# First block's mixer: half of the convolution moved from VectorE to ScalarE and Pool, rotary embedding from Pool to VectorE, and another order of the projections

## The chip, the core and the metric

The kernel runs on one core of a Trainium2 chip. The metric is the device time of one execution in microseconds; the number shown for a version is the median of its runs. The core has five instruction queues that run in parallel and meet at semaphores: TensorE (PE, with its weight loads as PEld), VectorE (DVE), ScalarE (ACT), GpSimd (POOL, "Pool" in the text) and SyncE (SP), which issues the transfers.

## What is computed

Two transformer blocks, each of two layers, on 256 tokens of 1024 features, in float32. The change lies in the mixer of the first block, which every one of its two layers runs between two feed-forward networks (FFN):

```python
def first_block(x, ...):
    for l in range(DEPTH):                                   # DEPTH = 2
        x = x + 0.5 * swiglu(rms_norm(x, ffn1_norm[l]), ...)
        h = rms_norm(x, mix_norm[l]) @ w_in[l]
        u_pool = h[..., OFF_POOL:OFF_MOBA]                   # 256 columns
        qm, km, vm = jnp.split(h[..., OFF_MOBA:OFF_DIL], 3, axis=-1)
        qd, kd, vd = jnp.split(h[..., OFF_DIL:OFF_CONV], 3, axis=-1)
        u_conv = h[..., OFF_CONV:]                           # 512 columns: a, g
        y_pool = pool_mixer(u_pool, pool_w[l], pool_scale[l])
        qm = apply_rope(to_heads(qm, MOBA_HEADS), cos, sin)  # and km, qd, kd
        y_moba = moba_attention(qm, km, vm)
        y_dil = dilated_attention(qd, kd, vd)
        y_conv = conv_module(u_conv, conv_w[l], conv_b[l], conv_ln_g[l], conv_ln_b[l])
        mix = jnp.concatenate([y_pool, y_moba, y_dil, y_conv], axis=-1)
        x = x + mix @ w_out[l]
        x = x + 0.5 * swiglu(rms_norm(x, ffn2_norm[l]), ...)
```

`conv_module` gates 256 channels, `a * sigmoid(g)`, convolves each over the tokens with 31 taps of its own, and ends with a layer norm and a SiLU. `apply_rope` turns 16 of the 64 features of each head of q and k. `pool_mixer` takes running means over 2, 4, 8 and 16 tokens.

## The kernel before

Weights come in transfers of 1 MB into one of three buffers `raw`, issued by SP in the order of the program. Each is split into two exact parts for TensorE: ACT copies `hi` (L210), DVE subtracts to get `lo` (L211), two pieces of 128x1024 for each transfer. A product of two split operands is three matmuls (`mm3`, L221 to L223). In almost all of the program TensorE runs these back to back, and the two splits run one or two transfers ahead of it.

`mixer1` (one call for each layer) projects the normed tokens. The outputs a and g of the convolution (`pa`, `pgc`) and the pool columns (`pp`) come feature-major, 128 features by 256 tokens, in `fm_pair`: 48 matmuls of 256 columns each. q and k of the one attention, q and k of the other and the v of both come token-major in three calls of `qkv_part(0)`, `(1)`, `(2)`: 48 matmuls of 512 columns each into two banks `pq`, which ACT evicts into `qkv` (L440). All of them take one of four banks of the pool `mmm`.

`scores` does one attention: rotary embedding in place on `qkv` in six Pool operations (L449 to L454), transposes of q and k (`pqk`, L459) evicted by ACT into `qkT` (L460), score products `ps` (L471) for the first and then the second 128 queries, and the softmax: DVE adds the mask into `e` (L478) and takes the maximum (L479), ACT takes the exponential (L481), DVE divides (L483, L484), TensorE transposes the weights (`ppt`, L490) and ACT evicts them (L491). There are two pieces of `ps` in the bank pool `mta`, so the second group of score products waits until DVE has read the first.

`conv_module` works on `hc`, two halves j of 128 channels with 256 tokens and 30 zeros ahead. A tap is one DVE operation `yc = hc * w + yc` on 128x256 (L553 the first, L555 the others). Of the second half's 31 taps the first eight are taken off DVE: ACT makes the product `pr` (L544, the first one straight into `yp`) and Pool adds it into `yp` (L547), with three buffers for `pr`; DVE adds `yp` in the end (L556).

`pool_mix` scales `pp` into `up` on DVE (L508), builds the window sums by doubling on Pool (L510, L512, L514, L516; tiles `s2`, `s4`, `s8`, `s16`, all named `s` in the rows), makes the means `pl` on Pool and DVE (L525 to L527), and TensorE multiplies each group with its matrix (`pps`, L533).

After the three projections the output projection `po` runs over the mixed columns `mixT`, whose last two column tiles come from the convolution. `block1` calls FFN, mixer, FFN for each layer.

Calls stand in the order of the code, but the order of instructions on each engine is set by a scheduler when the program is built: it moves independent work of several calls together, and then each engine runs its own list in order. An engine whose next instruction waits does nothing else.

Of the kernel before, what the change touches and what calls it, by code (L numbers as in the profile page):

```python
# [21 lines left out]
NPOOL, PRB = 8, 3  # L22
# [58 lines left out]
def _fm(w, n0, n1):  # L81
    """chunks of 256 columns: [chunk, 128, K / 128, 256]"""
    w = np.asarray(w)[:, n0:n1]
    return w.reshape(-1, 128, (n1 - n0) // 256, 256).transpose(2, 1, 0, 3)


def _tm(w, n0, n1, width=512):
    """column blocks, each with all its contraction tiles: [block, 128, K / 128, width]"""
    w = np.asarray(w)[:, n0:n1]
    return w.reshape(-1, 128, (n1 - n0) // width, width).transpose(2, 1, 0, 3)  # L90


# columns of w_in: q and k of both attentions of the first block, then their v
# [3 lines left out]
def _layout(inputs):  # L97
    """Arrays as the launch takes them: weights in the blocks that one transfer loads,
    small vectors as columns, the others as they come."""
# [50 lines left out]
def _build(ctx, tc, nc, V, A, P, T, a, out, col, ccol, stop):  # L150
# [29 lines left out]
    def C(name):  # L180
        lo, hi = ccol[name]
        return cst[:, lo:hi]
# [12 lines left out]
    def load_w(src, split=2):  # L195
        """src: DRAM view [128, a, b]; returns its exact parts hi + lo, both fp32r."""
# [20 lines left out]
    def mm3(ps, l, r, li, ri, start, stop):  # L217
        """ps += l^T r with the three leading partial products of the split operands."""
# [14 lines left out]
    def rsqrt(v, n, root=1.0):  # L233
        """root / sqrt(v) for n columns: seed y from the exponent, times two quadratics in t = v y^2
        whose product follows t^-1/2 to 3e-8 over the range of the seed."""
# [14 lines left out]
    def rstd(ssum, n, count, eps):  # L250
        """1 / sqrt(ssum / count + eps)"""
# [19 lines left out]
    # ================= block 1 =================  # L271
    class Norm1:
        """xT <- (x * g)^T split, one half of the columns after the other"""
# [25 lines left out]
        def finish(self):  # L299
            """the halves still to do; returns r columns and r along the free axis on all partitions"""  # L300
# [11 lines left out]
    def fm_pair(mm, w, mcols, n, name):  # L312
        """two feature-major output tiles of n tokens in one bank; w: chunk [128, 8, 256]."""
# [11 lines left out]
    def ffn1(norm, nxt, wg, wu, wd, l, after_mixer, nside=0, early=None, between=None):  # L325
        with ExitStack() as st:
            work = pool("fwork", 2, stack=st, side="right")
            hp = pool("fh", 1, stack=st, side="right")
            # banks 0 and 1, 2 to 5: what comes next begins in banks that are free by then
# [42 lines left out]
    # rope tables of block 1, token-major [128, 2, 8]  # L372
# [31 lines left out]
    def mixer1(norm, nxt, l):  # L404
        w_fm, w_tm, w_out = a["w_in_fm"][l], a["w_in_tm"][l], a["w_out"][l]
        with ExitStack() as st:
# [8 lines left out]
            # projections that stay feature-major: conv (a, g), pool  # L415
# [13 lines left out]
            # token-major projections: q and k of each attention, then v of both  # L429
# [13 lines left out]
            def scores(qo, mask, name):  # L443
                """transposed softmax weights: queries 128: see keys 0:128 and 128:256, queries 0:128 only the first"""
# [4 lines left out]
                P.tensor_tensor(rt[0], t1, cb, op=ALU.mult)  # L449
                P.tensor_tensor(rt[1], t2, sb, op=ALU.mult)  # L450
                P.tensor_tensor(rt[2], t2, cb, op=ALU.mult)
                P.tensor_tensor(rt[3], t1, sb, op=ALU.mult)
                P.tensor_tensor(t1, rt[0], rt[1], op=ALU.subtract)
                P.tensor_tensor(t2, rt[2], rt[3], op=ALU.add)  # L454
# [84 lines left out]
            def conv_module():  # L539
                yc = keep.tile([128, 2, 256], F32, name="yc")  # L540
                yp = keep.tile([128, 256], F32, name="yp")
                for t in range(NPOOL):
                    pr = work.tile([128, 256], F32, name="pr", bufs=PRB)
                    A.activation(pr if t else yp, hc[:, 1, t:t + 256], AF.Copy,  # L544
                                 scale=pcol("conv_w", (l * 31 + t) * 2 + 1))
                    if t:
                        P.tensor_tensor(yp, yp, pr, op=ALU.add)  # L547
                for j, t0 in ((0, 0), (1, NPOOL)):
                    for t in range(t0, 31):
                        w = pcol("conv_w", (l * 31 + t) * 2 + j)  # L550
                        src = hc[:, j, t:t + 256]
                        if t == t0:
                            V.tensor_scalar(yc[:, j], src, w, None, op0=ALU.mult)  # L553
                        else:
                            V.scalar_tensor_tensor(yc[:, j], src, w, yc[:, j], op0=ALU.mult, op1=ALU.add)  # L555
                V.tensor_tensor(yc[:, 1], yc[:, 1], yp, op=ALU.add)  # L556
# [30 lines left out]
            qkv_part(0)  # L587
            pp = fm_pair(mm, load_w(w_fm[2]), 0, 256, "pp")
            pt_moba = scores(0, C("causal"), "m")
            qkv_part(1)  # L590
# [7 lines left out]
            # output projection  # L598
# [34 lines left out]
    def setup():  # L633
        """what the first products do not need, in two steps"""
# [16 lines left out]
    def ada(l, v):  # L651
        """vector v of layer l, step by step: columns [128, k, stream], or gate * g rows in DRAM."""
# [17 lines left out]
        # row 32 (ns j + s): half j of stream s  # L670
# [40 lines left out]
    def tick(n, l=0):  # L711
        """n steps of the modulation of layer l, in the shade of the products."""
# [26 lines left out]
    # ================= block 2 =================  # L739
# [649 lines left out]
```

## Time and profile before

| | before |
| --- | --- |
| runs, us | 1941.36, 1938.75, 1937.58 |
| median, us | 1938.75 |
| the profiled execution: span from its first to its last instruction, us | 1936.9 |
| TensorE busy | 1897.2 us, 98% of the span |
| DVE busy | 1365.2 us, 70% |
| ACT busy | 952.5 us, 49% |
| Pool busy | 52.5 us, 3% |
| mean granted TensorE clock | 0.992 of full speed |

The page of the profiled execution gives only its span as its own time; it stands 1.85 us under the median of the runs. Busy shares are means over stages with different limits; the pages' slices show the clock of TensorE below full speed in one slice only, so what happens in a mixer of about 102 us is to be read from the timelines and waits of that stretch.

### The profile page before, as it was taken

To read this page: it belongs to the slowest core of one execution; us is meant where nothing else is said; L and a number is where in the kernel's file an instruction comes from. 1 tells how busy PE (TensorE), PEld (TensorE's weight loads), DVE (VectorE), ACT (ScalarE), POOL (GpSimd) and SP (SyncE) were. 2 spreads that over 40 slices of the span, in tenths; PEclk is the share of its full clock that TensorE was granted. 3 is DMA by queue.
4 is the path that set the end of the run, shared out by engine and by line. 5 is a ranking of instruction groups with operands and counts; after the bars stand their busy time and mean duration, and the time that the engine had idled before them with its cause. 6 is when DMAs were issued, how large, how long until landed. Compare 5 with 4: busy or idle time off the path is not lost.

```text
span 1936.9 us, 28694 instructions
## 1 busy us (share of the span) xinstructions
PE 1897.2 (98%) x11658; PEld 1638.5 (85%) x11658; DVE 1365.2 (70%) x2169; ACT 952.5 (49%) x1518; POOL 52.5 (3%) x96
## 2 busy tenths in 40 slices
PE   8999999999999998999999999999999999989998
PEld 8997879997999786899888767888878777669997
DVE  7777797777677769765544475795785787757774
ACT  5443555443444355644543475642432466766652
POOL 0000210000000012000000000000000001000000
PEclk9999999999999999999999999999999999989999
DMA  8667525667566752555533221355564532115552
GB/s 313 241 215 241 182 96 194 227 224 265 192 225 214 261 174 87 189 181 178 181 136 131 88 71 66 104 177 192 187 210 146 188 114 92 45 55 196 183 180 95
DMA packets 57419, 326.20 MB, mean 168 GB/s; under 512 B 6460, under 2 KB 6716, under 8 KB 26568
## 3 DMA queue, kind: packets, MB, share of 16 engines
q1 hardware_dynamic: 57288, 324.38, 49.0%
q8 instruction: 91, 1.49, 0.3%
q14 instruction: 40, 0.33, 0.1%
HBM read 323.29 MB, written 1.07 MB: 167 GB/s over the span
## 4 chain that ended last, share of the span: by engine, by line
PE 90%; DVE 5%; ACT 3%; issue 1%; POOL 0%; DMA 0%; SPq 0%; DVEq 0%; ACTq 0%
PE pg L221 8%; PE pg L223 7%; PE pg L222 7%; PE py L221 4%; PE py L223 4%; PE py L222 4%; PE pu L223 4%; PE pu L221 4%; PE pu L222 4%; PE pa L221 3%; PE pa L222 3%; PE pa L223 3%; PE pyd L221 3%; PE pyd L223 3%; PE pyd L222 3%; DVE yc L555 2%
## 5 line engine op out<-in xcount | busy, mean ns | idle before, releaser
L210 ACT ACTIVATE hi<-raw 128x1024 fp32r<-128x1024 f32 (+1 forms) x506 | 511.2, 1036 | 599.7 <-issue 143.7
L211 DVE TENSOR_TENSOR lo<-raw,hi 128x1024 fp32r<-128x1024 f32 (+1 forms) x506 | 600.5, 1204 | 243.8 <-ACT hi L210 243.8
L223 PE MATMUL pg<-xTh,lo 128*128 128x256 f32 (+1 forms) x1072 | 321.6, 300 | 0.4 <-DVE lo L211 0.4
L221 PE MATMUL pg<-xTh,hi 128*128 128x256 f32 (+1 forms) x1072 | 321.7, 300 | 0.2
L222 PE MATMUL pg<-xTl,hi 128*128 128x256 f32 (+1 forms) x1072 | 321.0, 300 | 0.0
L221 PEld LDWEIGHTS pg<-xTh,hi 128*128 128x128 f32 x1072 | 205.8, 192 | 9.7 <-issue 2.5
L223 PEld LDWEIGHTS pg<-xTh,lo 128*128 128x128 f32 x1072 | 205.5, 192 | 7.0 <-DVE lo L211 0.7
L222 PEld LDWEIGHTS pg<-xTl,hi 128*128 128x128 f32 x1072 | 205.6, 192 | 6.3
L222 PE MATMUL pu<-xTl,hi 128*128 128x256 f32 x704 | 199.4, 283 | 0.0
L221 PE MATMUL pu<-xTh,hi 128*128 128x256 f32 x704 | 199.3, 283 | 0.0
L223 PE MATMUL pu<-xTh,lo 128*128 128x256 f32 x704 | 199.2, 283 | 0.0
L664 DVE SCALAR_TENSOR_TENSOR aacc<-raw,sc_c,aacc 128x1024 f32<-128x1024 f32 x140 | 174.1, 1278 | 0.2
L221 PE MATMUL py<-hi,hTh 128*128 128x512 f32 x352 | 140.2, 398 | 0.0
L222 PE MATMUL py<-lo,hTh 128*128 128x512 f32 x352 | 139.7, 397 | 0.0
L223 PE MATMUL py<-hi,hTl 128*128 128x512 f32 x352 | 139.7, 397 | 0.0
L222 PEld LDWEIGHTS pu<-xTl,hi 128*128 128x128 f32 x704 | 135.1, 192 | 0.0
L223 PEld LDWEIGHTS pu<-xTh,lo 128*128 128x128 f32 x704 | 135.1, 192 | 0.0
L221 PEld LDWEIGHTS pu<-xTh,hi 128*128 128x128 f32 x704 | 135.1, 192 | 0.0
L222 PE MATMUL pa<-xTl,hi 128*128 128x256 f32 (+1 forms) x400 | 132.1, 330 | 0.1
L221 PE MATMUL pa<-xTh,hi 128*128 128x256 f32 (+1 forms) x400 | 131.6, 330 | 0.3
L223 PE MATMUL pa<-xTh,lo 128*128 128x256 f32 (+1 forms) x400 | 130.8, 327 | 0.0
L221 PE MATMUL pyd<-hi,chh 128*128 128x512 f32 (+1 forms) x286 | 108.8, 380 | 0.0
(368 smaller groups left out, 3426.0 us busy)
## 6 DMA issues: line engine op xcount, KB each, us to landing
raw<-in_w_ada SPq DMA_DIRECT2D x48, 1024.0 KB, 5.3
raw<-in_ffn_gate SPq DMA_DIRECT2D x44, 1024.0 KB, 4.9
raw<-in_ffn_up SPq DMA_DIRECT2D x44, 1024.0 KB, 5.0
raw<-in_w_up SPq DMA_DIRECT2D x44, 1024.0 KB, 4.8
raw<-in_ffn_down SPq DMA_DIRECT2D x40, 1024.0 KB, 5.0
raw<-in_w_down SPq DMA_DIRECT2D x18, 1024.0 KB, 5.1
raw<-in_w_in_tm SPq DMA_DIRECT2D x12, 1024.0 KB, 5.1
raw<-in_w_out SPq DMA_DIRECT2D x8, 1024.0 KB, 4.7
```

What stands on the lines that cost most here:

```text
L210: f = A.activation(hi[:, s], raw[:, s], AF.Copy)
L211: e = V.tensor_tensor(lo[:, s], raw[:, s], hi[:, s].bitcast(F32), op=ALU.subtract)
L221: f = T.matmul(ps, lh, rh, start=start, stop=False, skip_group_check=True)
L222: T.matmul(ps, lh, rl, start=False, stop=False, skip_group_check=True)
L223: e = T.matmul(ps, ll, rh, start=False, stop=stop, skip_group_check=True)
L555: V.scalar_tensor_tensor(yc[:, j], src, w, yc[:, j], op0=ALU.mult, op1=ALU.add)
L664: f = V.scalar_tensor_tensor(aacc[s], raw[:, k % 2], sc_c[:, s, k:k + 1], aacc[s], op0=ALU.mult, op1=ALU.add)
```

## The change

Three edits in `mixer1`. The second half of the convolution is now done by ACT and Pool alone: all 31 products come from ACT, Pool adds 30 of them straight into `yc[:, 1]`, and DVE does the 31 taps of the first half only. The rotary embedding is issued on DVE instead of Pool. And the calls stand in another order: q and k of both attentions are projected first, then come the scores of the first attention, and the projection of the pool columns (`pp`) only after that. Comments and docstrings are gone too, which shifts line numbers: L210, L211 are now L209, L210; L440, L460, L471 are L439, L459, L470; L544, L547 are L542, L545; L553, L555 are L550, L552; L533 is L532.

```diff
-NPOOL, PRB = 8, 3
...
                 rt = [work.tile([128, 2, 8, 8], F32, name=f"rt{i}", bufs=1) for i in range(4)]
-                P.tensor_tensor(rt[0], t1, cb, op=ALU.mult)
-                P.tensor_tensor(rt[1], t2, sb, op=ALU.mult)
-                P.tensor_tensor(rt[2], t2, cb, op=ALU.mult)
-                P.tensor_tensor(rt[3], t1, sb, op=ALU.mult)
-                P.tensor_tensor(t1, rt[0], rt[1], op=ALU.subtract)
-                P.tensor_tensor(t2, rt[2], rt[3], op=ALU.add)
+                V.tensor_tensor(rt[0], t1, cb, op=ALU.mult)
+                V.tensor_tensor(rt[1], t2, sb, op=ALU.mult)
+                V.tensor_tensor(rt[2], t2, cb, op=ALU.mult)
+                V.tensor_tensor(rt[3], t1, sb, op=ALU.mult)
+                V.tensor_tensor(t1, rt[0], rt[1], op=ALU.subtract)
+                V.tensor_tensor(t2, rt[2], rt[3], op=ALU.add)
...
             def conv_module():
                 yc = keep.tile([128, 2, 256], F32, name="yc")
-                yp = keep.tile([128, 256], F32, name="yp")
-                for t in range(NPOOL):
-                    pr = work.tile([128, 256], F32, name="pr", bufs=PRB)
-                    A.activation(pr if t else yp, hc[:, 1, t:t + 256], AF.Copy,
+                for t in range(31):
+                    pr = work.tile([128, 256], F32, name="pr", bufs=3)
+                    A.activation(pr if t else yc[:, 1], hc[:, 1, t:t + 256], AF.Copy,
                                  scale=pcol("conv_w", (l * 31 + t) * 2 + 1))
                     if t:
-                        P.tensor_tensor(yp, yp, pr, op=ALU.add)
-                for j, t0 in ((0, 0), (1, NPOOL)):
-                    for t in range(t0, 31):
-                        w = pcol("conv_w", (l * 31 + t) * 2 + j)
-                        src = hc[:, j, t:t + 256]
-                        if t == t0:
-                            V.tensor_scalar(yc[:, j], src, w, None, op0=ALU.mult)
-                        else:
-                            V.scalar_tensor_tensor(yc[:, j], src, w, yc[:, j], op0=ALU.mult, op1=ALU.add)
-                V.tensor_tensor(yc[:, 1], yc[:, 1], yp, op=ALU.add)
+                        P.tensor_tensor(yc[:, 1], yc[:, 1], pr, op=ALU.add)
+                for t in range(31):
+                    w = pcol("conv_w", (l * 31 + t) * 2)
+                    src = hc[:, 0, t:t + 256]
+                    if t == 0:
+                        V.tensor_scalar(yc[:, 0], src, w, None, op0=ALU.mult)
+                    else:
+                        V.scalar_tensor_tensor(yc[:, 0], src, w, yc[:, 0], op0=ALU.mult, op1=ALU.add)
...
             qkv_part(0)
+            qkv_part(1)
+            pt_moba = scores(0, C("causal"), "m")
             pp = fm_pair(mm, load_w(w_fm[2]), 0, 256, "pp")
-            pt_moba = scores(0, C("causal"), "m")
-            qkv_part(1)
             pool_mix(pp)
```

What the scheduler makes of it is seen in the engines' lists, at three places of the first layer's mixer. The first is ACT between the gate of the convolution and the softmax of the first attention. Before (`hi` are conversions of weights, `pr` products of the convolution, `qkv` and `qkT` the evictions):

```order
L544 ACTIVATE pr<-hc,par 128x256
L210 ACTIVATE hi<-raw 128x1024 x2
L544 ACTIVATE pr<-hc,par 128x256 x6
L440 ACTIVATE qkv<-pq,rs_2054 128x512 x2
L210 ACTIVATE hi<-raw 128x1024 x3
L460 ACTIVATE qkT<-pqk 128x4x128 x2
```

Now, on the same engine at the same place:

```order
L542 ACTIVATE pr<-hc,par 128x256
L209 ACTIVATE hi<-raw 128x1024 x2
L542 ACTIVATE pr<-hc,par 128x256 x7
L439 ACTIVATE qkv<-pq,rs_2054 128x512 x2
L209 ACTIVATE hi<-raw 128x1024 x2
L542 ACTIVATE pr<-hc,par 128x256 x8
L209 ACTIVATE hi<-raw 128x1024 x2
L542 ACTIVATE pr<-hc,par 128x256 x7
L439 ACTIVATE qkv<-pq,rs_2054 128x512 x2
L459 ACTIVATE qkT<-pqk 128x4x128 x2
```

Where seven products stood ahead of the first `qkT` there are 23 now, and the last seven stand right ahead of the second part's eviction.

The second place is DVE in the same stretch, from the tap that follows the gate on, as it is now:

```order
L210 TENSOR_TENSOR lo<-raw,hi 128x1024 x2
L552 SCALAR_TENSOR_TENSOR yc<-hc,par,yc 128x256 x6
L448 TENSOR_TENSOR rt_2327<-qkv,cs 128x128
L449 TENSOR_TENSOR rt_2328<-qkv,sn 128x128
L450 TENSOR_TENSOR rt_2329<-qkv,cs 128x128
L451 TENSOR_TENSOR rt_2330<-qkv,sn 128x128
L210 TENSOR_TENSOR lo<-raw,hi 128x1024
L452 TENSOR_TENSOR qkv<-rt_2327,rt_2328 128x2x8x8
L453 TENSOR_TENSOR qkv<-rt_2329,rt_2330 128x2x8x8
L210 TENSOR_TENSOR lo<-raw,hi 128x1024
L552 SCALAR_TENSOR_TENSOR yc<-hc,par,yc 128x256 x5
L210 TENSOR_TENSOR lo<-raw,hi 128x1024 x2
```

The rotary embedding has moved in between the taps, and six conversions `lo` stand in this piece, five of them behind the first.

The third place is Pool from the first sums of products on (`pe` are the heads of the means). Before:

```order
L547 TENSOR_TENSOR yp<-yp,pr 128x256 x7
L449 TENSOR_TENSOR rt_2316<-qkv,cs 128x128
L450 TENSOR_TENSOR rt_2317<-qkv,sn 128x128
L451 TENSOR_TENSOR rt_2318<-qkv,cs 128x128
L452 TENSOR_TENSOR rt_2319<-qkv,sn 128x128
L453 TENSOR_TENSOR qkv<-rt_2316,rt_2317 128x2x8x8
L454 TENSOR_TENSOR qkv<-rt_2318,rt_2319 128x2x8x8
L510 TENSOR_TENSOR s_2470<-up 128x2x271
L512 TENSOR_TENSOR s_2472<-s_2470 128x2x269
```

Now:

```order
L545 TENSOR_TENSOR yc<-yc,pr 128x256 x27
L509 TENSOR_TENSOR s_2470<-up 128x2x271
L545 TENSOR_TENSOR yc<-yc,pr 128x256
L511 TENSOR_TENSOR s_2472<-s_2470 128x2x269
L524 TENSOR_TENSOR pe_2479<-s_2470,cst 64x16
L545 TENSOR_TENSOR yc<-yc,pr 128x256
L513 TENSOR_TENSOR s_2474<-s_2472 128x265
L525 TENSOR_TENSOR pl<-pe_2479,up 64x16
L524 TENSOR_TENSOR pe_2483<-s_2472,cst 64x16
L545 TENSOR_TENSOR yc<-yc,pr 128x256
```

27 additions stand ahead of the pool sums, and three more between them. On TensorE the transposes `pqk` now follow 87 products `pq` without a break, then four products `pp` and the first score products; the pool products `pps` stand in the last projection as before, now with 38 of its 48 products behind them instead of 48. On SP the transfer of the pool columns' weights moves from ahead of the second q, k part to behind it.

## Rows read from the trace of the kernel before

**Rows 1.** The page: the span, and each engine's busy time in it.

```profile
span 1936.9 us, 28694 instructions
PE 1897.2 (98%) x11658; PEld 1638.5 (85%) x11658; DVE 1365.2 (70%) x2169; ACT 952.5 (49%) x1518; POOL 52.5 (3%) x96
```

**Rows 2.** TensorE's timeline in both mixers: start us, length, engine, line, names, count.

```profile
205.52 0.28 PE L221 MATMUL pa<-xTh,hi 128*128 128x256 f32 x1
...
220.77 0.40 PE L221 MATMUL pq<-hi,xTh 128*128 128x512 f32 x1
...
229.64 0.28 PE L221 MATMUL pp<-xTh,hi 128*128 128x256 f32 x1
...
260.77 1.08 PE L533 MATMUL pps<-pl,poolw 64*64 64x256 f32 x8
...
274.72 0.71 PE L471 MATMUL ps<-qkT 64*128 64x128 f32 x8 [0.19 <-ACT qkT L460]
...
307.86 0.28 PE L221 MATMUL pg<-xTh,hi 128*128 128x256 f32 x1
...
695.69 0.28 PE L221 MATMUL pa<-xTh,hi 128*128 128x256 f32 x1
...
797.06 0.28 PE L221 MATMUL pg<-xTh,hi 128*128 128x256 f32 x1
```

**Rows 3.** TensorE's waits, first mixer (two rows), then second: us, times, longest.

```profile
PE ps L471 <- DVE e L478: 2.9, 1, 2.9
PE pqk L459 <- POOL qkv L454: 2.2, 1, 2.2
...
PE ps L471 <- DVE e L478: 4.4, 1, 4.4
```

**Rows 4.** Windows: length, busy us (count) of five engines, TensorE clock, DMA share, GB/s.

```profile
238.50:241.80 3.30, 3.30 (x15) 2.33 (x14) 3.30 (x9) 3.19 (x4) 0.39 (x1) 0.50 0.63 191
...
245.30:252.00 6.70, 6.29 (x18) 4.80 (x19) 6.57 (x17) 3.73 (x16) 3.04 (x10) 0.50 0.00 0
...
733.40:740.10 6.70, 4.22 (x13) 3.21 (x14) 6.02 (x12) 1.77 (x9) 5.03 (x12) 0.50 0.00 0
```

**Rows 5.** DVE's timeline in the first mixer, where Pool stands: conversions and taps.

```profile
255.60 2.36 DVE L211 TENSOR_TENSOR lo<-raw,hi 128x1024 fp32r<-128x1024 f32 x2 [1.41 <-ACT hi L210]
257.88 4.04 DVE L555 SCALAR_TENSOR_TENSOR yc<-hc,par,yc 128x256 f32<-128x256 f32 x10
```

**Rows 6.** Pool's timeline in the first mixer, wide and in narrow windows: additions, then sums.

```profile
227.22 6.06 POOL L547 TENSOR_TENSOR yp<-yp,pr 128x256 f32<-128x256 f32 x6 [1.44 <-ACT pr L544]
...
228.13 2.49 POOL L547 TENSOR_TENSOR yp<-yp,pr 128x256 f32<-128x256 f32 x2
...
229.83 1.68 POOL L547 TENSOR_TENSOR yp<-yp,pr 128x256 f32<-128x256 f32 x2
...
230.71 1.69 POOL L547 TENSOR_TENSOR yp<-yp,pr 128x256 f32<-128x256 f32 x2
...
241.41 2.40 POOL L510 TENSOR_TENSOR s<-up 128x542 f32<-128x542 f32 x1 [3.74 <-DVE up L508]
243.89 1.08 POOL L512 TENSOR_TENSOR s<-s 128x538 f32<-128x538 f32 x1
...
245.27 0.62 POOL L514 TENSOR_TENSOR s<-s 128x265 f32<-128x265 f32 x1
...
248.36 0.51 POOL L526 TENSOR_TENSOR pl<-pe,up 64x16 f32<-64x16 f32 x2
```

**Rows 7.** ACT's timeline in the first mixer: product, evictions, last exponential.

```profile
229.78 0.51 ACT L544 ACTIVATE pr<-hc,par 128x256 f32<-128x256 f32 x1 [1.19 <-POOL yp L547]
...
231.08 1.25 ACT L440 ACTIVATE qkv<-pq,rs 128x512 f32<-128x512 f32 x2
...
238.42 1.29 ACT L460 ACTIVATE qkT<-pqk 128x512 f32<-128x512 f32 x2 [1.89 <-PE pqk L459]
...
283.68 0.50 ACT L481 ACTIVATE e<-e,mx 128x256 f32<-128x256 f32 x1
```

## Prediction, made before the changed kernel was run

> **What bounds the kernel now.** I read the page first, then TensorE's waits inside the two mixers, then the windows with their granted clock, and then the timelines of TensorE, Pool, DVE and ACT there. The span is 1936.9 us and TensorE is busy for 98% of it [rows 1], so a change pays only where TensorE idles or runs at half clock. In the first block's mixer it does both. The first mixer lasts from the first pa product at 205.52 to the first pg of the next FFN at 307.86, and the second from 695.69 to 797.06 [rows 2]. In each, two waits stand out: the transposes pqk wait 2.2 us for Pool's rotary embedding, and the second group of score products ps waits 2.9 us (4.4 us in the second mixer) for DVE's e [rows 3]. Around them the clock is at its lower level, 1.2 GHz, granted 0.50, in 3.3 and 6.7 us of the first mixer and 6.7 us of the second [rows 4]. TensorE was busy for 9.6 and 4.2 us of these, half of which is lost. So the waits cost about 5.1 + 4.8 = 9.9 us in the first mixer and 6.6 + 2.1 = 8.7 us in the second: the change can win 18.6 us at most.
>
> **What the change does, part by part.** The three edits pull at the same waits, so I follow the first mixer along its clock. Until 220.77 nothing differs.
>
> The order of projections: q and k of both attentions now run as one row of 87 products. Before, 39 such products took from 220.77 to 229.64, 0.2275 each [rows 2], so the row ends at 220.77 + 87 x 0.2275 = 240.6. Their weights come in time: the transfers change places on SP's queue with that of the pool projection, and the conversions (ACT hi, DVE lo) that fed pp at 229.64 feed the second q, k part, which is wanted at the same moment. Cost 0; if a conversion came late it would be one of some 1.2 us.
>
> Rotary embedding on DVE: six Pool operations go, and with them the 2.2 us wait for Pool, since they now run beside the products. DVE gets twelve operations on 128 elements in a mixer. No row has them; a tap of 256 elements takes 0.40 us alone (ten in 4.04 [rows 5]), so they lie between 0.1 and 0.4 each, and I take 0.2 as half the size: 2.4 us. DVE loses 23 taps and a sum, 24 x 0.40 = 9.6 us. So DVE as such gets lighter; I book 0, as the path goes by Pool.
>
> The convolution: ACT makes 31 products of the second half instead of 8, Pool adds 30 instead of 7. A product's buffer pr is one of three, so product t waits until Pool has added product t - 3; before, ACT already stood 1.19 us at such a product [rows 7]. In the order above, 23 products after the first now stand on ACT ahead of the eviction of q, k part 1 and of qkT, which the scores need. The 23rd needs the end of add 20.
>
> What an add takes, is what the sum hangs on. Beside taps the adds start 0.88 us apart (229.83, 230.71); where DVE runs a 128x1024 lo between, 1.70 apart (228.13, 229.83) [rows 6]. The nearest row for an undisturbed one is 0.62 for 265 elements [rows 6], which is the lower end. Pool and DVE evidently take turns. DVE now always has taps or lo in this stretch, so I take 0.88, and 0.82 more for each of the five lo that DVE's order sets between. Adds 2 to 20 start at 227.22 as before [rows 6]: 227.22 + 19 x 0.88 + 5 x 0.82 = 248.0. Then the last product, 0.5, the two evictions, 1.25, and half of the qkT pair, 0.65 [rows 7], less 0.1 of overlap: ps can start at 250.3. TensorE is through with q and k at 240.6, and with the transposes and the four pp that its order has ahead of ps some 1.3 later, at 241.9 (an estimate; 2 us more would shorten the wait, not move its end). So it idles **8.4 us** where it had idled 2.2 and 2.9.
>
> The second wait is new. The pool projection comes later, and on Pool the chain of window sums now stands behind add 27. Products 25 to 30 stand on ACT behind the softmax's exponentials. From the first ps to the end of the last exponential took 274.72 to 284.18 for the second attention [rows 2, 7], 9.5 us: 259.8. One product 0.5, adds 25 to 27 at 0.88: 262.9. The chain of sums itself took 241.41 to 248.87 [rows 6], 7.5 us; three more adds stand inside it, 2.6: 273.0. TensorE reaches the pool products pps earlier. From 250.3 it has left the scores, 44 pp at 0.12, ten pq at 0.23 and the transposes of the weights, some 13 us (an estimate: a pp is half as wide as a pq and takes half of 0.2275). So it stands another **8 to 10 us** with 38 products of the v projection behind pps that need nothing of it.
>
> From there on TensorE sets the pace as before. Before, from the end of pps at 261.85 to 307.86 [rows 2] took 46.0 us, with 48 pq behind; now 38 are left, 10 x 0.2275 = 2.3 less. The last two pps take 0.5: 273.5 + 43.7 = 317.2. That is **9.3 us later** than 307.86. Laid over the second mixer (490.17 later, ended at 306.89 on this clock) it is **10.3 us**. Together 19.6 us, and nothing outside the mixers moves.
>
> Here the Trainium skill speaks against the change. "SBUF — State Buffer", section "Who interferes with whom", states that a DVE instruction with two SBUF inputs and a GpSimd instruction that reads SBUF hold a shared port by turns, each for its whole instruction. The starts 0.88 us apart [rows 6] bear the turns out but not the whole length, since 0.40 and 0.62 alone would make 1.02. By 0.88 the sum stays as it is; by 1.02 it is that of the third rival.
>
> **The numbers.** The profiled execution spans 1936.9 us; the median of the runs is 1938.75, 1.85 more. 1936.9 + 19.6 + 1.85 = **1958.4 us**, slower by 1.0%. A measurement of this kernel tells some 0.2% (4 us) from no change.
>
> Bounds of this case: if two of the five lo fall where Pool is idle (1.6), no lo stands inside the softmax (1.2, two took 2.36 [rows 5]) and the three adds inside the sums cost nothing (2.6), a mixer ends 5.4 us earlier, 10.8 in all: 1947 or 1948. If the clock falls behind the second wait, as it did for 6.7 us behind the old ones [rows 4], up to 3.2 us are lost in each mixer: 1965. An error of 1 us in a mixer, from what I estimated, makes it 1967.
>
> **Rivals.** First, not slower: Pool's adds keep their own pace when they come in a long row. At 0.62, add 20 ends at 239.0, and ACT waits for TensorE instead: q and k end at 240.6, evictions and qkT follow, and ps starts at 242.5, 7.8 us earlier. The six adds that count after it give 1.6, and the sums, if nothing stretches them (the first took 2.40, a second of nearly the same size 1.08 [rows 6]), 1.3. The mixer ends at 306.5, 1.4 before today's, and the second 0.4 before: 1938.75 - 1.8 = 1937, no change. The point from which it decides is an average of some 0.65 us for an add, with no lo in its way. For it speaks that Pool's other operations are quick once DVE stands. Against it: DVE hardly stands between 225 and 243, and the adds of that stretch that follow on each other were at 0.88 or more. Chance 0.06.
>
> Second, worse than I say: the clock. Behind the first wait TensorE may stay at 1.2 GHz until pps. The 13 us of its work there become up to 26, so that it comes to pps at 276 rather than waiting for 273.0, and it loses 3.2 behind pps as well: 6.3 us in a mixer, 1971. The point is where its own arrival passes 273.0. For it: the wait of 8.4 us is nearly twice as long as the one of 4.4 that was followed by 6.7 us at half clock [rows 3, 4]. Against it: with work at hand, the full clock came back behind each of the old waits within that time. Chance 0.06.
>
> Third, the turns on the port are whole instructions: 1.02 for a pair of tap and add, 25 adds that count, 25 x 0.14 = 3.5 us in a mixer, 7.0 in all: 1965. Against it stand the starts at 0.88. Chance 0.03.
>
> Fourth, the edit does what its words say, the waits go, and TensorE runs through: 1938.75 - 18.6 = 1920. For that the pool sums would have to be done by some 256 on this clock. But add 25 stands behind exponentials that can't end before 242.5 + 9.5 = 252.0, and adds and sums take 10 us from there. Chance 0.03.
>
> **How the chances follow.** Main case 0.82, 1947 to 1967; first rival 0.06, second 0.06, third 0.03, fourth 0.03. The range of 1947 to 1968 holds the main case and the third rival, 0.85. Faster by over 0.2%: the fourth and a sixth of the first, 0.04. Within 0.2%: 0.05. Slower by over 0.2%: 0.91.
>
> **What would show it.** Right: in TensorE's waits of each mixer ps stands behind ACT's qkT for some 8 us, and pps behind DVE's or Pool's pl for some 8; in ACT's timeline the products of line 542 wait for Pool again and again; Pool's adds start 0.88 apart, 1.7 where a lo falls; DVE's taps beside them start 0.88 apart rather than 0.40; the mixers last about 112 us instead of 102. Wrong: adds 0.62 apart with DVE busy, or ps starting before 243, or no wait at pps.

## The result, and the profile after

The changed kernel takes 1967.77 us (median; 1966.77 to 1968.13) against 1940.05 us for the kernel before in the same comparison: a ratio of 1.0143, with a 95% interval of [1.0128, 1.0157]. It is **slower by 27.7 us**. Forecast were 19.6 us and a range of 1947 to 1968: the direction is right, the time lies 0.2 us inside the range's upper end, and 8 us of the effect are missing from the sum.

The page of the profiled execution after, its span and first row of busy times (before: [rows 1]):

```profile
span 1966.2 us, 28777 instructions
...
PE 1908.5 (97%) x11658; PEld 1645.7 (84%) x11658; DVE 1367.2 (70%) x2145; ACT 972.9 (49%) x1564; POOL 79.2 (4%) x118
```

The span grew by 29.3 us, but TensorE's busy time by 11.3 only, with the same 11658 matmuls: most of the loss is idling, and the rest matmuls that ran slower. DVE is as busy as before with fewer instructions, which will matter below. TensorE's waits within the first mixer (the second mixer's answer has the same two rows with the same numbers):

```profile
PE ps L470 <- ACT qkT L459: 9.0, 1, 9.0
PE pps L532 <- POOL pl L525: 6.2, 3, 4.9
```

These are the two waits that were forecast, where [rows 3] had 5.1 us in the first mixer and 6.6 in the second. TensorE's timeline places them:

```profile
207.18 0.28 PE L220 MATMUL pa<-xTh,hi 128*128 128x256 f32 x1
...
252.67 1.22 PE L470 MATMUL ps<-qkT 64*128 64x128 f32 x8 [8.98 <-ACT qkT L459]
...
271.22 1.11 PE L532 MATMUL pps<-pl,poolw 64*64 64x256 f32 x2 [4.87 <-POOL pl L525]
...
275.51 1.41 PE L532 MATMUL pps<-pl,poolw 64*64 64x256 f32 x4 [0.18 <-POOL pl L525]
...
322.33 0.28 PE L220 MATMUL pg<-xTh,hi 128*128 128x256 f32 x1
...
710.08 0.28 PE L220 MATMUL pa<-xTh,hi 128*128 128x256 f32 x1
...
826.01 0.28 PE L220 MATMUL pg<-xTh,hi 128*128 128x256 f32 x1
```

The first mixer lasts 115.15 us (102.34 before) and the second 115.93 (101.37): 12.8 and 14.6 us more, together 27.4. All but 1.9 us of the 29.3 is in the mixers; 1.66 of the rest lies ahead of the first one, where the code is the same, and is not explained. The windows of these mixers in which the granted clock is 0.50, which is 1.2 GHz (columns as in [rows 4]):

```profile
248.50:258.80 10.30, 6.13 (x27) 5.04 (x28) 10.01 (x20) 8.87 (x19) 4.45 (x7) 0.50 0.30 103
269.00:279.20 10.20, 6.64 (x15) 3.30 (x16) 6.35 (x10) 2.29 (x4) 6.21 (x13) 0.50 0.00 1
750.30:760.50 10.20, 4.93 (x21) 3.83 (x22) 9.90 (x18) 8.30 (x18) 5.24 (x6) 0.50 0.30 103
770.80:784.40 13.60, 9.45 (x21) 5.53 (x22) 8.65 (x12) 2.59 (x5) 6.81 (x13) 0.50 0.08 13
```

Around the end of each wait the clock is at 1.2 GHz for 10.2 us or more: it falls while TensorE still waits (248.50, the wait ends at 252.67) and comes back 6 us or so behind the first wait. Half of the busy time in these windows is lost: (6.13 + 6.64) / 2 = 6.4 and (4.93 + 9.45) / 2 = 7.2 us, where [rows 4] gave 4.8 and 2.1. So of 27.4 us, the waits explain 2 x 15.2 - 11.7 = 18.7, the clock around them 13.6 - 6.9 = 6.7, and 2.0 are smaller things.

What ends the first wait. ACT's timeline (in brackets: idle before, and who ended it):

```profile
241.04 0.51 ACT L542 ACTIVATE pr<-hc,par 128x256 f32<-128x256 f32 x1 [1.17 <-POOL yc L545]
...
250.47 0.51 ACT L542 ACTIVATE pr<-hc,par 128x256 f32<-128x256 f32 x1 [0.36 <-POOL yc L545]
250.88 1.25 ACT L439 ACTIVATE qkv<-pq,rs 128x512 f32<-128x512 f32 x2
252.02 1.08 ACT L459 ACTIVATE qkT<-pqk 128x512 f32<-128x512 f32 x2
```

ACT waits for Pool at product after product, and qkT, which needs nothing of the convolution, stands behind them and the two evictions in its list. Pool's timeline of the same stretch, and on to the window sums:

```profile
228.88 7.00 POOL L545 TENSOR_TENSOR yc<-yc,pr 128x256 f32<-128x256 f32 x7 [1.44 <-ACT pr L542]
237.36 8.02 POOL L545 TENSOR_TENSOR yc<-yc,pr 128x256 f32<-128x256 f32 x8 [1.48 <-ACT pr L542]
245.74 7.29 POOL L545 TENSOR_TENSOR yc<-yc,pr 128x256 f32<-128x256 f32 x7 [0.36 <-ACT pr L542]
...
263.36 2.89 POOL L545 TENSOR_TENSOR yc<-yc,pr 128x256 f32<-128x256 f32 x3 [4.13 <-ACT pr L542]
266.21 1.09 POOL L509 TENSOR_TENSOR s<-up 128x542 f32<-128x542 f32 x1
...
274.37 1.38 POOL L525 TENSOR_TENSOR pl<-pe,up 64x16 f32<-64x16 f32 x2
```

And DVE in that stretch:

```profile
227.64 2.35 DVE L210 TENSOR_TENSOR lo<-raw,hi 128x1024 fp32r<-128x1024 f32 x2
229.91 5.37 DVE L552 SCALAR_TENSOR_TENSOR yc<-hc,par,yc 128x256 f32<-128x256 f32 x6
...
244.72 3.40 DVE L210 TENSOR_TENSOR lo<-raw,hi 128x1024 fp32r<-128x1024 f32 x2
...
254.44 0.74 DVE L477 SCALAR_TENSOR_TENSOR e<-ps,cst 128x256 f32<-128x256 f32 x2
```

No row of DVE between these shows idle time: it went from the conversions at 227.64 to the mask e at 254.44 without a stop. The scores start at 252.67. So two engines are late by nearly the same amount, ACT with qkT and DVE with e, and the trace of this one kernel can't tell which of them sets the time, or why.

### The profile page after: what moved, and what is told of

Its sections match the earlier page's. It is cut to its first block, busy times and chain, and to the rows that moved or that the text cites. A ratio compares the mean times of both kernels' runs of the same rounds, so it can differ in the third digit from the quotient of the medians.

```text
span 1966.2 us, 28777 instructions
## 1 busy us (share of the span) xinstructions
PE 1908.5 (97%) x11658; PEld 1645.7 (84%) x11658; DVE 1367.2 (70%) x2145; ACT 972.9 (49%) x1564; POOL 79.2 (4%) x118
## 4 chain that ended last, share of the span: by engine, by line
PE 93%; ACT 2%; DVE 2%; POOL 2%; issue 1%; DMA 0%; SPq 0%; DVEq 0%; ACTq 0%; POOLq 0%
PE pg L220 7%; PE pg L222 7%; PE pg L221 7%; PE pu L222 4%; PE pu L220 4%; PE pu L221 4%; PE py L220 4%; PE py L222 4%; PE py L221 4%; PE pa L220 3%; PE pa L221 3%; PE pa L222 3%; PE pyd L220 3%; PE pyd L222 3%; PE pyd L221 3%; PE po L222 2%
## 5 line engine op out<-in xcount | busy, mean ns | idle before, releaser
L209 ACT ACTIVATE hi<-raw 128x1024 fp32r<-128x1024 f32 (+1 forms) x506 | 510.9, 1036 | 590.9 <-issue 138.0
L210 DVE TENSOR_TENSOR lo<-raw,hi 128x1024 fp32r<-128x1024 f32 (+1 forms) x506 | 601.5, 1206 | 254.0 <-ACT hi L209 253.7
```

What stands on the lines that cost most here:

```text
L209: f = A.activation(hi[:, s], raw[:, s], AF.Copy)
L210: e = V.tensor_tensor(lo[:, s], raw[:, s], hi[:, s].bitcast(F32), op=ALU.subtract)
```

## The experiments

**Theory T**, from the prediction: Pool's 30 additions, slowed by turns with DVE, hold up ACT's list and the window sums behind them. Rivals: **R1**, the new order of the projections costs the time; **R2**, ACT's 31 products themselves are too much; **R3**, the half clock is a cause of its own. The kernel before took 1940.05 to 1940.63 us in these comparisons; differences are against the value of the same comparison.

| run | what it is | us | ratio to before, 95% interval | difference |
| --- | --- | --- | --- | --- |
| | the change | 1967.77 | 1.0143 [1.0128, 1.0157] | +27.7 |
| e1 | convolution alone | 1956.16 | 1.0084 [1.0069, 1.0099] | +16.1 |
| e6 | rotary embedding alone | 1947.40 | 1.0038 [1.0025, 1.0051] | +7.1 |
| e7 | order alone | 1949.59 | 1.0047 [1.0032, 1.0062] | +9.3 |
| e2 | rotary embedding and order | 1952.59 | 1.0067 [1.0052, 1.0082] | +12.5 |
| e10 | convolution and rotary embedding | 1951.46 | 1.0055 [1.0041, 1.0069] | +10.8 |
| e3 | the change, 29 additions out | 1939.32 | 0.9998 [0.9988, 1.0007] | -0.8 |
| e4 | the change, 30 taps out | 1963.21 | 1.0118 [1.0101, 1.0135] | +23.1 |
| e5 | the change, one product for all | 1976.90 | 1.0188 [1.0173, 1.0203] | +36.6 |
| e9 | e5, sum kept apart | 1967.34 | 1.0136 [1.0122, 1.0150] | +26.7 |
| e8 | the change, pool mixing later | 1958.16 | 1.0091 [1.0074, 1.0107] | +17.9 |
| e11 | before, 3 products instead of 8 | 1936.10 | 0.9977 [0.9967, 0.9986] | -4.5 |
| e12 | before, e6 and pool mixing later | 1936.15 | 0.9977 [0.9968, 0.9986] | -4.5 |

**e1, the convolution's edit in the kernel before; e2, all of the change but that edit.** In e1 the loops of the convolution are those of the change; in e2 they are those of before, and the rest is as changed.

> The kernel before with the convolution's edit alone (31 products on ACT, 30 additions on Pool); rotary embedding on Pool and the old order of projections. Theory T (the row of additions on Pool, slowed by turns with DVE, holds up ACT's list and the work behind it on Pool): TensorE waits longer for the first scores (qkT stands behind 15 products instead of 7, the rotary embedding behind 8 additions) and again at the pool products, slower than before by 8 to 16 us: 1948 to 1956. Rival R1 (the new order of projections is what costs): within 4 us of the kernel before. Rival R2 (ACT's load of products, not Pool): also slower, but then ACT is busy, not waiting for Pool, ahead of the first qkT.

> The changed kernel with the convolution of before (8 products, 7 additions, the rest on DVE): rotary embedding on DVE and the new order stay. T: the wait of 9.0 us for the first scores goes (ACT has only 7 products there), to 2 us or less. The pool columns are still projected late, and DVE now has its 53 taps and sum again, so a wait at the pool products stays, some 3 to 8 us in each mixer: 1942 to 1953. R1 (order): as the changed kernel, 1960 or more, with the wait for the first scores too. If the two edits merely add, e1 and this one together are 27.7 us over the kernel before.

TensorE's waits in the first mixer, e1, and after it e2:

```profile
PE ps L471 <- ACT qkT L460: 7.5, 2, 4.2
PE pqk L459 <- POOL qkv L454: 3.9, 1, 3.9
```

```profile
PE ps L471 <- DVE e L478: 3.7, 1, 3.7
PE pps L533 <- POOL pl L526: 3.4, 2, 2.3
```

e1 went a little past T's range. The waits for the rotary embedding and for the first scores are those that T named, but there is none at the pool products: of the 7.5 us, 3.3 are the first attention's and 4.2 the second's, whose qkT is late too. e2's time lies within T's range; the wait of the first scores for qkT is gone, as T said, and the 3.7 us are the second group's wait for DVE's e, 2.9 and 4.4 us in the kernel before [rows 3]. So the convolution's edit is the larger half, and R1 holds in part: the order and the rotary embedding cost 12.5 us without it. 16.1 and 12.5 make 28.6, close to 27.7; that this is no law shows below (e10).

**e3, the additions taken out.** ACT makes its 31 products as before.

```diff
                     if t:
-                        P.tensor_tensor(yc[:, 1], yc[:, 1], pr, op=ALU.add)
+                        if t < 2: P.tensor_tensor(yc[:, 1], yc[:, 1], pr, op=ALU.add)
```

> The changed kernel; Pool makes only the first of the 30 additions, so 29 products of the second half of the convolution are made by ACT and left out of the sum. ACT's load is the same. T: no product waits for Pool, so the 23 products end by 241 or so, the first scores wait 2 us or less instead of 9.0, and the pool sums start as soon as they have their columns; the wait at the pool products is halved at least. 1940 to 1950. R2 (ACT's 31 products of 0.5 us themselves are too much): the wait for the first scores stays at 6 us or more, 1958 or more. R3 (the half clock itself is the main cost): no other result than T, but per mixer the stretches at half clock shrink by more than the waits do.

The time is that of the kernel before, a little under T's range. TensorE's waits and, of DVE's timeline, the same operations as above:

```profile
PE pps L532 <- POOL pl L525: 3.9, 3, 2.2
PE ps L470 <- DVE e L477: 0.8, 1, 0.8
```

```profile
226.64 2.35 DVE L210 TENSOR_TENSOR lo<-raw,hi 128x1024 fp32r<-128x1024 f32 x2
228.91 3.08 DVE L552 SCALAR_TENSOR_TENSOR yc<-hc,par,yc 128x256 f32<-128x256 f32 x6
...
237.87 2.36 DVE L210 TENSOR_TENSOR lo<-raw,hi 128x1024 fp32r<-128x1024 f32 x2
...
244.35 0.74 DVE L477 SCALAR_TENSOR_TENSOR e<-ps,cst 128x256 f32<-128x256 f32 x2
```

R2 falls: 31 products on ACT cost nothing where nobody makes them wait. For R3, the windows at 0.50 that are left (first and second mixer):

```profile
259.70:263.10 3.40, 3.31 (x9) 2.16 (x10) 1.68 (x4) 1.87 (x3) 0.25 (x2) 0.50 0.00 0
747.80:754.70 6.90, 6.51 (x16) 4.68 (x17) 4.71 (x8) 2.53 (x4) 0.55 (x2) 0.51 0.01 4
```

R3's sign is there: the waits fell by 10.5 us in each mixer (15.2 to 4.7), the stretches at 0.50 by 17 (20.5 to 3.4, and 23.8 to 6.9). But what these stretches cost, half of TensorE's busy time in them, fell by 4.7 and 3.9 us only, and each of them lies around the end of a wait. So the low clock adds to what a wait costs; that it is the main cost, or a cause without a wait, no run shows.

Without Pool's 29 additions nothing of the net loss is left. That isn't to say that the order costs nothing (3.9 us of wait at the pool products stay): DVE has 24 operations of the convolution less in a mixer than in the kernel before, against twelve short ones of the rotary embedding, and its e is waited for 0.8 us instead of 2.9. DVE also shows more than T asked: the 34 operations from the conversion pair to e take 17.7 us here (226.64 to 244.35) and 26.8 with the additions (227.64 to 254.44). Six taps need 3.08 us instead of 5.37, two conversions 2.36 instead of 3.40. Pool's row slows DVE.

**e4, the taps taken out.** Does DVE slow Pool as much?

```diff
-                        V.scalar_tensor_tensor(yc[:, 0], src, w, yc[:, 0], op0=ALU.mult, op1=ALU.add)
+                        pass
```

> The changed kernel; DVE makes only the first tap of the first half of the convolution, 30 are left out. Pool's 30 additions and ACT's 31 products stay. T (turns between DVE and Pool set the pace): additions where DVE stands come 0.62 us apart, 1.4 to 1.7 where a conversion lo runs; the 20th ends near 242 to 244, so the first scores wait some 2 to 5 us instead of 9.0, and the pool products 1 to 4 instead of 6.2. 1943 to 1955. Rival: an addition in a row with a product takes 0.88 us by itself, whatever DVE does: starts stay 0.88 apart and the time at 1962 or more.

It doesn't. Here is Pool's timeline in a narrow window where DVE stands still, the end of DVE's stand (in brackets), and TensorE's waits:

```profile
241.65 3.17 POOL L545 TENSOR_TENSOR yc<-yc,pr 128x256 f32<-128x256 f32 x4
```

```profile
244.73 2.89 DVE L210 TENSOR_TENSOR lo<-raw,hi 128x1024 fp32r<-128x1024 f32 x2 [4.57 <-ACT hi L209]
```

```profile
PE ps L470 <- ACT qkT L459: 8.4, 1, 8.4
PE pps L532 <- POOL pl L525: 5.2, 3, 3.2
```

Four additions, with 0.74 for the last (one alone takes that), leave (3.17 - 0.74) / 3 = 0.81 from start to start, not the 0.62 that T expected. That is near the 0.88 of this run's rival, whose time (1962 or more) it is too. A tap beside an addition costs Pool only 0.07 us more. The turns with taps, which were to explain the 0.88, are not the cause; 0.81 of it is Pool's own pace. Conversions do hold Pool up: in the change's ACT rows above, the wait of 1.17 instead of 0.36 ahead of 241.04 is the addition that ran beside a lo.

**e5 and e9, ACT freed from Pool.** ACT makes two products; Pool adds the second one 30 times, in e5 into yc, in e9 into a tile of its own.

```diff
 e5
-                    pr = work.tile([128, 256], F32, name="pr", bufs=3)
-                    A.activation(pr if t else yc[:, 1], hc[:, 1, t:t + 256], AF.Copy,
-                                 scale=pcol("conv_w", (l * 31 + t) * 2 + 1))
+                    if t < 2:
+                        pr = work.tile([128, 256], F32, name="pr", bufs=3)
+                        A.activation(pr if t else yc[:, 1], hc[:, 1, t:t + 256], AF.Copy,
+                                     scale=pcol("conv_w", (l * 31 + t) * 2 + 1))
 e9, besides
+                yp = keep.tile([128, 256], F32, name="yp")
...
-                        P.tensor_tensor(yc[:, 1], yc[:, 1], pr, op=ALU.add)
+                        P.tensor_tensor(yp, pr, pr, op=ALU.add) if t == 1 else P.tensor_tensor(yp, yp, pr, op=ALU.add)
```

> The changed kernel; ACT makes the first product and one more, and Pool adds that one 30 times, so 29 products are left out. Pool's load stays, ACT no longer waits for Pool. T in its two parts (Pool holds up ACT's list, which makes the wait for the first scores; Pool's own list makes the wait at the pool products): the wait for the first scores goes to 2 us or less; the additions, 0.81 apart and 1.6 where a lo runs, take from 229 to some 256, the window sums come behind them, and the pool products, which TensorE now reaches some 8 us earlier, wait 5 to 9 us. 1946 to 1957. Rival: all of the delay is in ACT's list: both waits small, 1944 or less. And of the additions: if a product on ACT beside them is what makes 0.73 of 0.62, they are 0.62 here.

e5 lies 20 us past its range. ACT's timeline shows why, and Pool's beside it gives an undisturbed row, since ACT and DVE both stand:

```profile
255.07 0.51 ACT L555 ACTIVATE yc<-yc,par 128x256 f32<-128x256 f32 x1 [21.43 <-POOL yc L546]
```

```profile
247.92 7.12 POOL L546 TENSOR_TENSOR yc<-yc,pr 128x256 f32<-128x256 f32 x9
```

With its products gone, the scheduler moved the closing operation of the convolution, which needs the 30th addition, ahead of q, k part 1 on ACT, and the first scores waited 16.0 us. This is the first wait's mechanism at nearly twice its size: one instruction on ACT that waits for Pool's row holds up a qkT that doesn't need it. And with no product and no tap beside them, nine additions of 0.72 are (7.12 - 0.72) / 8 = 0.80 us apart. The Trainium skill, "Perfetto Trace Analysis", section "GPSIMD Engine Instruction", advises to time such operations from start to start, since the reported span is unreliable; here the two differ, 0.80 and 0.72.

> e5 again, with Pool's 30 additions of the one product kept in a tile of their own that nobody reads, so that no evicting instruction of ACT stands behind them; 29 products and the sum are left out. Theory T2 (what e1 to e8 leave: ACT's list behind Pool's row makes the first wait; Pool's row itself delays the window sums): the wait of 9.0 us for the first scores goes to 2 us or less. The additions take from 227 to some 256, near the time when the pool columns are ready, so the pool products wait about as in e3, 3 to 6 us. 1938 to 1948. If Pool's row costs by itself and not through ACT's list: the pool products wait 7 us or more, 1952 or more.

e9 misses too, and it settles the open point. TensorE's waits:

```profile
PE ps L470 <- DVE e L477: 13.4, 1, 13.4
PE pps L532 <- POOL pl L525: 3.4, 2, 2.4
```

The time is still that of the change, though ACT is on time; its eviction of q and k:

```profile
243.06 1.08 ACT L459 ACTIVATE qkT<-pqk 128x512 f32<-128x512 f32 x2
```

Now it is DVE that comes late; DVE's timeline:

```profile
227.61 3.44 DVE L210 TENSOR_TENSOR lo<-raw,hi 128x1024 fp32r<-128x1024 f32 x2
...
258.06 0.74 DVE L477 SCALAR_TENSOR_TENSOR e<-ps,cst 128x256 f32<-128x256 f32 x2
```

The same 34 operations take 30.45 us beside an unbroken row of additions, 12.7 more than in e3. (The change's row has gaps, and its DVE list takes 26.8; so e9 makes DVE later than the change does.) So T was half of it. **Pool's row holds the scores twice**: through ACT's list (e4, where DVE has the conversions and little else to do, still waits 8.4 us for qkT) and through DVE's (e9, where ACT waits for nothing of Pool's, waits 13.4 us for e). Either alone gives most of the loss, which is why taking away one gives 4.6 or 1.0 us and taking away the additions gives 28.5. The Trainium skill, "Perfetto Trace Analysis", section "Optimizing Scalar/DVE Operations", says that moving work between DVE and GpSimd may not help because they share a read port; these runs agree, with 12.7 us more for the same DVE list. That the port is the reason, no run here shows.

**e6 and e7, the other two edits alone** (six P. to V. in `scores`; the four moved lines in `mixer1`).

> The kernel before with the rotary embedding on DVE alone. It takes the wait of 2.2 us for Pool away and puts twelve operations (0.28 to 0.87 us) behind taps on DVE, whose e the second group of scores waited for already. If the 12.5 us that rotary embedding and order cost together (e2) come from DVE's load: 1944 to 1953 with a longer wait for DVE's e. If they come from the order: 1936 to 1942.

> The kernel before with the new order of projections alone, rotary embedding on Pool, convolution as before. The pool columns come later, so pps should wait 2 to 5 us for Pool's window sums in each mixer, with about 7 us at half clock behind it; the wait of the transposes for Pool's rotary embedding goes. If the order is what costs in e2: 1946 to 1953. If DVE's load with the rotary embedding does: 1938 to 1944.

The longest wait of e6, and the two waits of e7, in the first mixer:

```profile
PE ps L471 <- DVE e L478: 4.0, 1, 4.0
```

```profile
PE ps L471 <- DVE e L478: 6.2, 1, 6.2
PE pps L533 <- POOL pl L526: 3.1, 2, 2.1
```

Both costs are real, so it was not one or the other. e6's other waits of over 1 us are for DVE as well (1.9, 1.4 and 1.3 us). The order makes a wait at pps of 3.1 us by itself, with the short row of 7 additions, and it is still 3.9 in e3 without any row: the late pool projection alone makes a wait of half the second one's size or more. And in the old work split DVE, with 54 taps of the convolution, is the engine that the softmax waits for.

**e8, the second wait alone.**

```diff
             pp = fm_pair(mm, load_w(w_fm[2]), 0, 256, "pp")
+            qkv_part(2)
             pool_mix(pp)
-            qkv_part(2)
```

> The changed kernel with the pool columns' mixing written behind the v projection instead of ahead of it: the pool products come later in TensorE's list. T: the wait for the first scores is untouched, 8 to 9.5 us; the wait of 6.2 us at the pool products and the half clock behind it go or shrink to a third, 1954 to 1962. If the clock behind the first wait alone makes the second (TensorE late anyway): 1964 or more.

```profile
PE ps L470 <- ACT qkT L459: 9.0, 1, 9.0
PE pqk L458 <- DVE xTl L535: 5.1, 1, 5.1
```

The first wait is the same, the one at pps is gone, and 9.8 us with it, as T said, although a wait of 5.1 us for DVE appears at the transposes of the second attention.

**e10, the change without its order.**

> The kernel before with the convolution and the rotary embedding of the change, in the old order of projections. Alone they cost 16.0 and 7.1 us (e1, e6). T2: the rotary embedding on DVE takes away the wait of 3.9 us behind Pool's additions (e1), and DVE has room for it now that 24 of its operations are gone; qkT still stands behind 15 products. So less than their sum: 1946 to 1956. If the costs merely add: 1961 to 1965.

```profile
PE ps L471 <- ACT qkT L460: 4.1, 1, 4.1
PE ps L471 <- DVE e L478: 3.3, 2, 1.7
```

10.8 us is less than the convolution alone costs (16.1): the edits don't add. The rotary embedding costs 7.1 us while DVE is full and gains 5.2 once the convolution has left DVE: e1's wait of 3.9 us for Pool's rotary embedding, behind the additions, is one of 1.6 for DVE's here. The order, 9.3 alone, costs 16.9 on top of both others.

**e11 and e12, the other way.** NPOOL is 3 instead of 8 in e11. e12 is e6 with the two lines of e8 changed places.

> The opposite of the change: the kernel before with 3 products on ACT and 2 additions on Pool instead of 8 and 7, five more taps on DVE (2 us at 0.40 in each mixer). T2: Pool's rotary embedding starts earlier and the wait of 2.2 us for it shrinks; DVE's e, for which the second group of scores waits, comes about as late or later. 1935 to 1941. If DVE's taps set the pace: slower by 2 to 6 us, 1942 to 1946.

> The kernel before with the rotary embedding on DVE (e6, slower by 7.1 us) and the mixing of the pool columns written behind the v projection (as e8 did to the changed kernel). T2: DVE's operations of the pool columns leave the stretch where the softmax of the first attention needs DVE, so the loss of e6 goes and the wait for Pool's rotary embedding goes with it: 1933 to 1941. If the late pool products make TensorE wait at the output projection instead: 1944 or more.

Both beat the kernel before by 4.5 us, and the change by 32. In e11 the wait for Pool's rotary embedding (2.2 in [rows 3]) is gone though DVE has five taps more; in e12 1.3 us of it are left, for DVE. The wait for e, 2.9 in the first mixer before, is 4.4 and 4.0 us there. So the waits don't show what the 4.5 us are: those of the first mixer sum to 6.4 and 6.9 us against 5.5 before, and why these two are faster stays open. Whether the two gains add was not tried.

## Why the prediction was right, and where it was off

The mechanism that was forecast is there: Pool's additions hold up ACT's list (e4, e5) and the window sums behind them (e8 takes that wait away), at the places and nearly at the times of the sum. Half of it was missed, DVE's list, and the time lies in the range partly by luck, as follows.

- **The adds' pace**: 0.88 apart is what Pool's groups show beside taps, and add 20, the fourth of the group that starts at 245.74, ends at 250.4; the program began its first mixer 1.66 us later than before (207.18 against 205.52), which leaves 248.8 on the old clock against 248.0 forecast. That is luck in part. The sum had 4.1 us for five lo; three of them stretched an addition (ACT's waits of 1.08, 1.17 and 1.16 us instead of 0.36), which makes some 2.3, and Pool stood 1.48 and 0.36 us for ACT's products, which the sum hadn't. The reason given was wrong for the 0.88: "Pool and DVE evidently take turns" explains 0.07 of it with a tap (e4, e5); 0.80 is Pool's own. With a lo it stands: 1.68. The first rival's 0.62, from the nearest row of 265 elements, was no price for these additions.
- **The first wait**: 9.0 us against 8.4, ps at 251.0 on the old clock against 250.3. ACT ends it, as said.
- **DVE "gets lighter; I book 0"** failed as a reason. Its list became as late as ACT's, since taps beside additions take 0.88 instead of 0.40 to 0.52 and conversions 1.7 instead of 1.2. It cost nothing extra only because ACT was late by as much. That the taps would slow was written down among the signs; the sum didn't follow it to e.
- **The order, booked at 0**: e7 and e2 show 9.3 and 12.5 us. In the sum its cost went under the second wait, so the end was near all the same, which is luck.
- **The second wait**: 6.2 us instead of 8 to 10. TensorE came to pps 1.4 us later than forecast (266.35, 264.7 on the old clock, against 263.3), 0.7 of it from the first wait, though 6.1 us of the work between ran at 1.2 GHz. And it waited in three pieces: four pps and a pq ran between them, 3.0 us, so that 9.2 us passed from its arrival to the last start of pps, as long as forecast. The last pps starts at 273.85 on the old clock against 273.0 forecast.
- **The term that was mis-sized is the clock**, which the sum left out and the bounds put at up to 3.2 us in a mixer. Behind the last start of pps, its last products took 1.41 us instead of 0.5, and the way to pg 45.4 instead of 43.7: 2.6 of the 3.5 us by which the first mixer ended later than forecast. The windows show the low level up to 279.2 there, 3.7 us behind that start, so half of these, 1.8, are the clock's and 0.8 stay open. In the second mixer, 4.3 us later than forecast, the low level lasts 6.5 us behind the last start of pps (777.90 to 784.40), 3.3 lost. That is what the bounds allowed for, so the range held and the sum didn't. The second rival put the clock at 6.3 us in a mixer, with a wait at pps that vanishes; it stayed.
- **The port as whole instructions** (third rival): a tap and an addition together would make at least 0.80 + 0.40 = 1.20; 0.88 was measured.

## What to carry to other kernels

Work moved to an idle engine is paid for on the engines that feed it and on those whose operations it slows: price it by the start-to-start time of the nearest row in place, and look at what stands behind it in both lists. When two engines are late by the same amount, taking the blame from either changes little; only an experiment that removes the common cause shows its size. And a wait of TensorE should be booked with the stretch at 1.2 GHz around its end: here 30.4 us of waits brought 13.6 us more.

## What was unexpected of the hardware

- An addition of 128x256 on Pool is 0.80 us from start to start with nothing beside it, 0.88 beside a tap and about 1.68 beside a 128x1024 conversion. The tap grows from 0.40 to 0.52 [rows 5, and e3] to 0.88, the conversion from 1.2 to 1.7. The loss isn't shared evenly: between taps and additions nearly all of it falls on DVE, between conversions and additions more on Pool.
- 1.2 GHz set in while TensorE still stood in its two long waits of each mixer and stayed 6.1 us behind the end of the first (252.67) and 8.0 behind the first start of pps (271.22); in the second mixer it was 4.9 and 10.8. Behind the ends of the waits of 2.9 and 4.4 us in the kernel before it was 6.3 and 4.2. Of the two waits of 2.2 us there, the first mixer's had 3.3 us of it behind it and the second's none [rows 3, 4].
